# Seven quadrant products for eight in the gate and up projections, with the down projection as a stage behind them

## The chip, the cores and the metric

The kernel runs on one core of one Trainium2 chip. The time is the device time of one execution in microseconds, the median of three runs. The engines are named as in the profile: PE is the matrix engine (PEld its weight load), DVE the vector engine, ACT the scalar engine, POOL the GpSimd engine, SP the engine whose queue issues nearly all the DMAs. The change touches only the last part of the kernel, the feed-forward network; the output projection before it is touched where it hands over.

## What is computed

The block ends with a residual feed-forward network on 1024 tokens (the meta tokens are dropped before it) of width 1024, with an inner width of 2816, in float32:

```
hs  = hs + mixer_block(rmsnorm(hs, norm_mix), ...)
h   = rmsnorm(hs, norm_ffn)
hs  = hs + (silu(h @ w_gate) * (h @ w_up)) @ w_down     # w_gate, w_up: 1024 x 2816, w_down: 2816 x 1024
out = rmsnorm(hs, norm_final)
```

## The kernel before

**Arithmetic.** Each float32 operand of a matmul is held as two tiles, a rounded high part (`wh`, `oph`) and the rest (`wl`, `opl`). One product is three matmuls: high by high, high by low, low by high (`mm3`, which records its matmuls on L196). So a PSUM group of 512 columns that contracts over 1024 takes 8 x 3 = 24 matmuls of 128x128 by 128x512.

**Weights.** `plan` lists the weight blocks in the order of use. `next_w` keeps one block loaded ahead; `load_w` fetches a block of 1024 x 256 in two DMAs of 512 KB into the two `wraw` tiles (L136), rounds it on ACT into `wh` (L138), and subtracts on POOL (first half) and DVE (second half) into `wl` (L139). `wh` and `wl` have two buffers each.

**Hand-over.** In the last quarter of the output projection (`b == 3`, matmuls on L1058, 256 columns) every finished row tile `hs[i]` of 128 tokens gets its sum of squares (ACT, L246) and its scale (POOL, L118 and L119), and DVE writes the scaled copy into an `act` tile (L1034). `norm2_cols` transposes four of these tiles for one of the eight column blocks into a `tp` bank of PSUM (L1042; there are two such banks), and ACT and DVE evict it into a pair `oph`, `opl` (L1044, L1045). The first four row tiles are done inside the output projection; the other four come behind the first 24 matmuls of the feed-forward network.

**Feed-forward.** Eleven steps `s` of 256 inner columns. `gate_up(s)` makes four groups for gate and four for up (two column blocks `j`, two token halves `hh`). The gate groups leave through Silu on ACT into `fsg` (L1089); the up groups are multiplied with these on DVE (L1094), rounded on ACT (L1095) and the rest subtracted on DVE (L1096) into the `act` tiles, which hold all 1024 tokens. `down(s - 1)` follows each `gate_up(s)`: 16 groups of 6 matmuls (L1107), each added on DVE into `hs`, which stays in SBUF (L1109). PSUM groups go round six banks (`pc`: `mm`, `yo`, `ss`, `cb`, `yo`, `yd`). A scheduler sets the order on each engine from the program; `tc.issue_after` holds an instruction behind another.

Of the kernel before, what the change touches and what calls it, by code (L numbers as in the profile page):

```python
# [15 lines left out]
P = 128  # L16
# [41 lines left out]
def tile_hybrid_block(  # L58
# [32 lines left out]
    d_a = dram.tile([KC, P, T], F32, name="d_a")  # L91

# [48 lines left out]

    def next_w(key):

        while plan and len(ready) < 2:
            k, view, lo = plan.pop(0)
            ready.append((k, load_w(view, lo)))
        k, w = ready.pop(0)
        assert k == key, (k, key)
        return w
# [868 lines left out]
    hsp = ctx.enter_context(tc.tile_pool(name="hs", bufs=1))  # L1018
# [3 lines left out]
    h2 = [None] * (2 * KC)  # L1022
    xn = [None] * NTT
    ffp = ctx.enter_context(tc.tile_pool(name="ffp", bufs=2))

    def row_tile():
        return ffp.tile([P, D], F32, name="act", tag="act", bufs=8)

    todo = []

    def norm2_rows(i, added):
        if i:
            with tc.issue_after(added.ins):
                V.tensor_scalar(out=xn[i - 1][0], in0=hs[i - 1], scalar1=xn[i - 1][1], scalar2=None, op0=ALU.mult)  # L1034
        if i < NTT:
            t = row_tile()
            xn[i] = t, rms_stat(t, hs[i], P)

    def norm2_cols(half, k):
        ps = pb("tp")  # L1040
        for i in range(4):
            PE.transpose(ps[:, i * P:(i + 1) * P], xn[4 * half + i][0][:, k * P:(k + 1) * P], ident)  # L1042
        hi, lo = h2[half * KC + k] = op_tile()
        S.activation(out=hi, in_=ps, func=AF.Copy, scale=prm(R_NF, k))  # L1044
        V.scalar_tensor_tensor(out=lo, in0=ps, scalar=prm(R_NF, k), in1=hi.bitcast(F32),  # L1045
                               op0=ALU.mult, op1=ALU.subtract)

    for b in range(4):
        wh, wl = next_w(f"o{b}")
        for i in range(NTT):  # L1050
            ps = pc()
            sl = slice(i % 4 * P, (i % 4 + 1) * P)
            if b == 3 and i == 6:
                todo = list(range(KC))
            for k in range(KC):
                mh, ml = mop[i // 4 * KC + k]
                for q_, (a, bb) in enumerate(((mh, wh), (mh, wl), (ml, wh))):
                    PE.matmul(ps[:, :256], lhsT=a[:, sl], rhs=bb[:, k, :], start=(k == 0 and q_ == 0),  # L1058
                              stop=(k == KC - 1 and q_ == 2))
                if todo and k % 2:  # L1060
                    norm2_cols(0, todo.pop(0))
# [5 lines left out]
    todo = list(range(KC))  # L1067


    def gate_up(s):  # L1070
        res = [[row_tile().bitcast(F32R) for _ in range(2)] for _ in range(2)]
        sgs = []
        for key in ("wg", "wu"):
            wh, wl = next_w(f"{key}{s}")
            for hh in range(2):
                ts = halves(hh)
                for j in range(2):
                    js = slice(j * P, (j + 1) * P)
                    ps = pc()
                    o = h2[hh * KC:(hh + 1) * KC]  # L1080
                    mm3(ps, [wh[:, k, js] for k in range(KC)], [wl[:, k, js] for k in range(KC)],
                        [t[0] for t in o], [t[1] for t in o])
                    if todo:
                        with tc.issue_after(last_mm[0].ins):
                            while todo:
                                norm2_cols(1, todo.pop(0))
                    if key == "wg":
                        sg = ffp.tile([P, 512], F32, name="fsg", bufs=6)
                        S.activation(out=sg, in_=ps, func=AF.Silu)  # L1089
                        sgs.append(sg)  # L1090
                        continue
                    sg = sgs.pop(0)
                    ah, al_ = res[j]
                    V.tensor_tensor(out=sg, in0=ps, in1=sg, op=ALU.mult)  # L1094
                    S.copy(out=ah[:, ts], in_=sg)  # L1095
                    V.tensor_tensor(out=al_[:, ts], in0=sg, in1=ah[:, ts].bitcast(F32), op=ALU.subtract)  # L1096
        return res

    def down(s, res, after=None):
        wh, wl = next_w(f"wd{s}")  # L1100
        for i in range(NTT):
            sl = slice(i * P, (i + 1) * P)
            for t0, n in HALF:
                ps = pc()
                for k in range(2):
                    for q_, (a, bb) in enumerate(((res[k][0], wh), (res[k][0], wl), (res[k][1], wh))):
# [76 lines left out]
```

## Time and profile before

| | |
|---|---|
| median of three runs | 2297.45 us (2295.74 to 2298.12) |
| the profiled execution's own time | 2297.74 us |
| its span, first to last instruction | 2295.9 us |
| PE / DVE / ACT / POOL busy | 2228.8 / 1383.9 / 764.4 / 846.0 us |
| mean granted PE clock | 0.991 of full speed |

A busy share is a mean over the whole span. The feed-forward network is the last third of the span, from 1550.67 us on; the part of it that changes runs to 2243.97 us, the start of the last down step, which stays as it is.

### The profile page before, as it was taken

Reading aid. Unit: us, or ns where it says so; the run is one execution under the profiler, and the core shown is the slowest. Engines: PE = TensorE matmul, PEld = TensorE weight load, DVE = VectorE, ACT = ScalarE, POOL = GpSimd, SP = SyncE. Lnnn points to the kernel's source line nnn. Section 1 sums busy time; section 2 is a strip of 40 time slices with the busy share of each in tenths; the row PEclk is TensorE's granted clock in tenths of the full one; section 3 lists DMA queues with packets and bytes.
Section 4 is the critical chain, followed back from the end, with each engine's and each line's share of the span. In section 5 each row is a group of like instructions: output and inputs, shape, how many; then the busy total and the mean of one; then the engine's idle time right before and its main releaser. Section 6 shows DMA issues by size and latency. Waiting matters only on the chain.

```text
span 2295.9 us, 30987 instructions
## 1 busy us (share of the span) xinstructions
PE 2228.8 (97%) x12103; PEld 1903.6 (83%) x12103; DVE 1383.9 (60%) x1726; ACT 764.4 (33%) x1386; POOL 846.0 (37%) x729
## 2 busy tenths in 40 slices
PE   7999999999999999988999999999999999999998
PEld 7999999999997766665677788998888888888886
DVE  4389898997871587887997664533332333433236
ACT  6333342322322454545555462223111111111112
POOL 3374664821202586867785510111010110101102
PEclk9999999999999999999999999999999999999999
DMA  4222222232236675746753752411111111111111
GB/s 140 85 76 67 83 70 71 86 119 99 89 109 202 195 209 164 226 142 209 229 169 119 241 159 84 147 38 52 41 56 37 55 39 53 55 37 56 37 55 73
DMA packets 223162, 245.29 MB, mean 107 GB/s; under 512 B 19113, under 2 KB 174361, under 8 KB 223017
## 3 DMA queue, kind: packets, MB, share of 16 engines
q1 hardware_dynamic: 210200, 221.89, 31.3%
q10 hardware_dynamic: 12816, 21.44, 2.5%
q8 instruction: 95, 1.56, 0.3%
q14 instruction: 51, 0.41, 0.1%
HBM read 174.23 MB, written 69.04 MB: 106 GB/s over the span
## 4 chain that ended last, share of the span: by engine, by line
PE 48%; DMA 2%; DVE 2%; ACT 1%; POOL 1%; issue 1%; SPq 0%; POOLq 0%; DVEq 0%; ACTq 0%
PE yo L196 11%; PE mm L196 9%; PE ss L196 4%; PE yd L196 4%; PE cb L196 4%; PE yo L1107 3%; PE ss L1107 2%; PE cb L1107 2%; PE yd L1107 2%; DMA wraw<-d_vn 1%; PE mm L1107 1%; PE yo L1058 1%; PE cb L1058 1%; PE ss L1058 1%; PE mm L1058 1%
## 5 line engine op out<-in xcount | busy, mean ns | idle before, releaser
L139 POOL TENSOR_TENSOR wl<-wraw,wh 128x1024 fp32r<-128x1024 f32 (+1 forms) x103 | 249.9, 2436 | 1080.0 <-ACT wh L138 1079.8
L196 PE MATMUL mm<-hnh,wh 128*128 128x352 f32 (+4 forms) x1208 | 410.6, 340 | 14.9 <-ACT w L553 13.5
L196 PE MATMUL mm<-hnh,wl 128*128 128x352 f32 (+4 forms) x1208 | 403.8, 334 | 2.8 <-POOL wl L139 2.8
L196 PE MATMUL mm<-hnl,wh 128*128 128x352 f32 (+4 forms) x1208 | 405.8, 336 | 0.4 <-DVE hnl L378 0.4
L138 ACT CAST wh<-wraw 128x1024 fp32r<-128x1024 f32 (+1 forms) x172 | 175.0, 1042 | 420.3 <-PE yd L1107 175.5
L139 DVE TENSOR_TENSOR wl<-wraw,wh 128x1024 fp32r<-128x1024 f32 x69 | 139.2, 2020 | 252.6 <-ACT wh L138 247.8
L196 PEld LDWEIGHTS mm<-hnh,wh 128*128 128x128 f32 x1208 | 228.3, 189 | 29.9 <-ACT w L553 17.5
L474 DVE SCALAR_TENSOR_TENSOR acc<-ap,pr,acc 128x1024 f32<-128x1024 f32 x192 | 247.5, 1289 | 6.3
L196 PEld LDWEIGHTS mm<-hnh,wl 128*128 128x128 f32 x1208 | 228.3, 189 | 12.9 <-POOL wl L139 3.4
L196 PEld LDWEIGHTS mm<-hnl,wh 128*128 128x128 f32 x1208 | 228.2, 189 | 9.8 <-issue 1.2
L474 DVE SCALAR_TENSOR_TENSOR acc<-xp,pr,acc 128x1040 f32<-128x1040 f32 x120 | 156.6, 1305 | 4.0
L196 PE MATMUL mm<-oph,wh 128*128 128x512 f32 x344 | 139.5, 405 | 11.9 <-ACT w L656 9.9
L272 PE MATMUL mm<-wh,hnh 128*128 128x256 f32 x512 | 144.7, 283 | 5.1 <-ACT w L275 5.1
L272 PE MATMUL mm<-wl,hnh 128*128 128x256 f32 x512 | 144.6, 283 | 0.0
L272 PE MATMUL mm<-wh,hnl 128*128 128x256 f32 x512 | 144.5, 283 | 0.0
L196 PE MATMUL mm<-opl,wh 128*128 128x512 f32 x344 | 137.1, 398 | 3.0 <-DVE opl L623 3.0
L196 PE MATMUL yo<-oph,wh 128*128 128x512 f32 x352 | 139.0, 395 | 0.0
L196 PE MATMUL yo<-opl,wh 128*128 128x512 f32 x352 | 138.9, 395 | 0.0
L196 PE MATMUL yo<-oph,wl 128*128 128x512 f32 x352 | 138.8, 394 | 0.0
L196 PE MATMUL mm<-oph,wl 128*128 128x512 f32 x344 | 136.7, 397 | 0.0
L758 POOL TENSOR_SCALAR_AFFINE_SELECT sel<-adh 128x512 fp32r<-128x512 f32 x128 | 98.7, 792 | 70.8 <-ACT wh L138 41.6
L513 POOL TENSOR_TENSOR tap<-tap 128x1024 f32<-128x1024 f32 x40 | 96.1, 2403 | 34.4 <-ACT tap L509 33.3
(316 smaller groups left out, 4938.8 us busy)
## 6 DMA issues: line engine op xcount, KB each, us to landing
wraw<-in_w_in_dram SPq DMA_DIRECT2D x72, 512.0 KB, 3.7
xc<-d_x SPq DMA_DIRECT2D x64, 256.0 KB, 3.5
wraw<-in_w_gate_dram SPq DMA_DIRECT2D x22, 512.0 KB, 4.7
wraw<-in_w_up_dram SPq DMA_DIRECT2D x22, 512.0 KB, 3.8
wraw<-in_w_down_dram SPq DMA_DIRECT2D x22, 512.0 KB, 3.7
d_x<-xa ACTq DMA_DIRECT2D x16, 520.0 KB, 2.6
d_sz<-w ACTq DMA_DIRECT2D x64, 128.0 KB, 2.1
d_xt<-xt SPq DMA_DIRECT2D x32, 256.0 KB, 3.3
```

The lines of the kernel that those rows point to most:

```text
L138: S.copy(out=h3[:, sl], in_=r3)
L139: (V if lo[i] == "v" else GP).tensor_tensor(out=l3[:, sl], in0=r3, in1=h3[:, sl].bitcast(F32), op=ALU.subtract)
L196: tie(PE.matmul(out_, **kw))
L272: PE.matmul(ps[:, :256], lhsT=a[:, sl], rhs=bb[:, k, :], start=(k == 0 and q_ == 0), stop=(k == KC - 1 and q_ == 2))
L474: V.scalar_tensor_tensor(out=out_ if last else acc, in0=sl(k), scalar=w(k), in1=acc, op0=ALU.mult, op1=ALU.add)
L513: GP.tensor_tensor(out=t, in0=t, in1=part, op=ALU.add)
L758: GP.affine_select(out=dst, in_=hbc(src, self.c, h0, 4, P, P), pattern=[[0, 4], [-1 if back else 1, P]], compare_op=ALU.is_ge, fill=0.0, b ...
L1058: PE.matmul(ps[:, :256], lhsT=a[:, sl], rhs=bb[:, k, :], start=(k == 0 and q_ == 0), stop=(k == KC - 1 and q_ == 2))
L1107: PE.matmul(ps, lhsT=a[:, sl], rhs=bb[:, k, t0:t0 + n], start=(k == 0 and q_ == 0), stop=(k == 1 and q_ == 2))
```

## The change

Gate and up. Step 0 is still computed with 24 matmuls for each group (`gate_up_plain`). In steps 1 to 10 a weight block is cut into four quadrants (`A11`, `A21`, `A12`, `A22`: two column blocks by two halves of the contraction) and the normalized activations into four (`B11`, `B21`: token half 0, `B12`, `B22`: token half 1, by the halves of the contraction). Strassen's scheme in Winograd's form gives the four results from seven products of quadrants, each contracting over 512, so of 4 x 3 = 12 matmuls (`wino`). It needs four sums of weight quadrants (`S1` to `S4`, made anew for each block in `load_wino`, all four by POOL), four of activation quadrants (`T1` to `T4`, made once at the hand-over in `norm2_second` and `norm2_last`), and sums of the products, which DVE adds as it evicts them (`plus`). Seven pairs are rounded and split for each block where `load_w` split 2 halves of a block.

Down. The gated result goes to memory (`d_act`); the loads of `wd` move in `plan` behind all gate and up blocks; `load_act` reads the result back in pieces of 128x512 and splits it there. `hs` is written to memory unscaled (`d_hs`), scaled in place for the transposes, its place given to other tiles, and it is read back for the down stage.

```diff
+    def load_wino(view):
+        fa = fa_box[0]
+        raws = []
+        for i in range(2):
+            raw = wts.tile([P, 1024], F32, name="wraw", tag="wraw", bufs=2)
+            r3 = raw.rearrange("p (a b) -> p a b", b=256)
+            SP.dma_start(out=r3, in_=view[:, 4 * i:4 * i + 4, :])
+            raws.append(r3)
+        a11, a21, a12, a22 = (raws[h][:, :, j * P:(j + 1) * P] for h in range(2) for j in range(2))
...
+            if name in ("S3", "A22", "S4"):
+                pair = tuple(fa.tile([P, 512], F32R, name=n_, bufs=3) for n_ in ("yah", "yal"))
+            else:
+                pair = slots.pop(0)
+            h, l = (k4(t) for t in pair)
+            S.copy(out=h, in_=src)
+            eng.tensor_tensor(out=l, in0=src, in1=h.bitcast(F32), op=ALU.subtract)
+            res[name] = h, l
+
+        s1 = k4(fa.tile([P, 512], F32, name="s1", bufs=1))
+        split_q("A11", a11, V)
+        split_q("A12", a12, V)
+        GP.tensor_tensor(out=s1, in0=a21, in1=a22, op=ALU.add)
+        GP.tensor_tensor(out=a21, in0=a11, in1=a21, op=ALU.subtract)
+        GP.tensor_tensor(out=a11, in0=s1, in1=a11, op=ALU.subtract)
+        split_q("S2", a11, V)
+        split_q("S1", s1, GP)
+        GP.tensor_tensor(out=a12, in0=a12, in1=a11, op=ALU.subtract)
+        split_q("S3", a21, V)
+        split_q("A22", a22, GP)
+        split_q("S4", a12, GP)
+        return res
...
-        add_plan(f"wg{i}", w_gate[0], 256 * i, LOD)
-        add_plan(f"wu{i}", w_up[0], 256 * i, LOD)
-        if i:
-            plan_down(i - 1)
-    plan_down(NFF // 2 - 1)
+        add_plan(f"wg{i}", w_gate[0], 256 * i, None if i else LOD)
+        add_plan(f"wu{i}", w_up[0], 256 * i, None if i else LOD)
+    for i in range(NFF // 2):
+        plan_down(i)
...
         if i:
             with tc.issue_after(added.ins):
-                V.tensor_scalar(out=xn[i - 1][0], in0=hs[i - 1], scalar1=xn[i - 1][1], scalar2=None, op0=ALU.mult)
+                V.tensor_scalar(out=hs[i - 1], in0=hs[i - 1], scalar1=rsx[i - 1], scalar2=None, op0=ALU.mult)
         if i < NTT:
...
+            SP.dma_start(out=d_hs[i], in_=hs[i])
+            rsx[i] = rms_stat(fx.tile([P, D], F32, name="t2", bufs=2), hs[i], P)
...
+    def norm2_second(k):
+        ps = norm2_cols(1, k)
+        b12 = B["B12", k] = split_cols(ps, k, x_pair("x", 4))
+        h11, l11 = (t.bitcast(F32) for t in B["B11", k])
+        t1 = fx.tile([P, 512], F32, name="t1", bufs=2)
+        V.scalar_tensor_tensor(out=t1, in0=ps, scalar=prm(R_NF, k), in1=h11, op0=ALU.mult, op1=ALU.subtract)
+        V.tensor_tensor(out=t1, in0=t1, in1=l11, op=ALU.subtract)
+        B["T1", k] = split_t(op_tile(), t1, GP)
+        ps = norm2_cols(1, k + 4)
+        B["B22", k] = split_cols(ps, k + 4, op_tile())
...
+        V.scalar_tensor_tensor(out=t2, in0=ps, scalar=prm(R_NF, k + 4), in1=t1, op0=ALU.mult, op1=ALU.subtract)
+        B["T2", k] = split_t(x_pair("y", 8), t2, GP)
+        t3 = fx.tile([P, 512], F32, name="t3", bufs=2)
+        V.scalar_tensor_tensor(out=t3, in0=ps, scalar=prm(R_NF, k + 4), in1=b12[0].bitcast(F32), op0=ALU.mult,
+                               op1=ALU.subtract)
+        V.tensor_tensor(out=t3, in0=t3, in1=b12[1].bitcast(F32), op=ALU.subtract)
+        B["T3", k] = split_t(x_pair("y", 8), t3, GP)
+
+    def norm2_last(k):
+        t2 = t2f[k + 1]
+        h21, l21 = (t.bitcast(F32) for t in B["B21", k])
+        GP.tensor_tensor(out=t2, in0=h21, in1=t2, op=ALU.subtract)
+        V.tensor_tensor(out=t2, in0=t2, in1=l21, op=ALU.add)
+        B["T4", k] = split_t(x_pair("x", 4), t2, V)
...
+    def act_out(s, j, hh, ps_or_sum, sg):
+        V.tensor_tensor(out=sg, in0=ps_or_sum, in1=sg, op=ALU.mult)
+        SP.dma_start(out=d_act[2 * s + j, :, halves(hh)], in_=sg)
...
+    def wino(key, emit):
+        w = next_w(key)
+
+        def prod(a, b):
+            ps = pc()
+            h, l = w[a]
+            for k in range(4):
+                bh, bl = B[b, k]
+                for q_, (x_, y_) in enumerate(((h, bh), (h, bl), (l, bh))):
+                    matmul(ps, lhsT=x_[:, k, :], rhs=y_, start=(k == 0 and q_ == 0), stop=(k == 3 and q_ == 2))
+            return ps
...
+        S.copy(out=u, in_=prod("A11", "B11"))
+        emit(0, 0, plus(prod("A12", "B21"), u))
+        plus(prod("S2", "T2"), u, u)
+        u3 = plus(prod("S3", "T3"), u)
+        ps = prod("S1", "T1")
+        emit(1, 1, plus(ps, u3))
+        plus(ps, u, u)
+        emit(1, 0, plus(prod("A22", "T4"), u3, u3))
+        emit(0, 1, plus(prod("S4", "B22"), u, u))
...
+    def load_act(s):
+        res = {}
+        for hh in range(2):
+            for j in range(2):
+                h, l = res[j, hh] = op_tile()
+                SP.dma_start(out=l.bitcast(F32), in_=d_act[2 * s + j, :, halves(hh)])
+                S.copy(out=h, in_=l.bitcast(F32))
+                (V, GP)[j].tensor_tensor(out=l, in0=l.bitcast(F32), in1=h.bitcast(F32), op=ALU.subtract)
+        return res
...
-    prev = None
     for s in range(NFF // 2):
-        res = gate_up(s)
-        if prev is not None:
-            down(s - 1, prev)
-        prev = res
-    down(NFF // 2 - 1, prev, final_norm)
+        nxt = load_act(s + 1) if s + 1 < NFF // 2 else None
+        down(s, res, None if nxt else final_norm)
+        res = nxt
```

The scheduler places the added work. On DVE at the hand-over, from the scaling of the sixth row tile on, the rows before were these (`hs_14371` is the last row tile):

```order
L1034 TENSOR_SCALAR act<-hs_14370,rs 128x1024
L1045 SCALAR_TENSOR_TENSOR opl<-tp,pr,oph 128x512
L1034 TENSOR_SCALAR act<-hs_14371,rs 128x1024
L139 TENSOR_TENSOR wl<-wraw,wh 128x1024
L1045 SCALAR_TENSOR_TENSOR opl<-tp,pr,oph 128x512 x8
L139 TENSOR_TENSOR wl<-wraw,wh 128x1024
```

The same place after the change (`hs_14376` is the last row tile; `t_15437` is a `t1`, `t_15453` a `t2`, `t_15459` a `t3`; `xh`, `xl` are the pair of `B12`):

```order
L141 TENSOR_TENSOR wl<-wraw,wh 128x1024
L1084 TENSOR_SCALAR hs_14376<-hs_14376,rs 128x1024
L1097 SCALAR_TENSOR_TENSOR xl<-tp,pr,xh 128x512
L1117 SCALAR_TENSOR_TENSOR t_15437<-tp,pr,oph 128x512
L1118 TENSOR_TENSOR t_15437<-t_15437,opl 128x512
L1097 SCALAR_TENSOR_TENSOR opl<-tp,pr,oph 128x512
L1125 SCALAR_TENSOR_TENSOR t_15453<-tp,pr,t_15437 128x512
L1128 SCALAR_TENSOR_TENSOR t_15459<-tp,pr,xh 128x512
L1097 SCALAR_TENSOR_TENSOR xl<-tp,pr,xh 128x512
L1130 TENSOR_TENSOR t_15459<-t_15459,xl 128x512
L1117 SCALAR_TENSOR_TENSOR t_15475<-tp,pr,oph 128x512
L1138 TENSOR_TENSOR t_15453<-t_15453,opl 128x512
```

Eight evictions of `tp` in a row have become a series in which a `tp` bank is read by two or three DVE instructions, with additions between SBUF tiles among them; the weight split (L139, now L141) now stands ahead of the scaling of the last row tile. On PE the eight transpose groups of the second half, which stood within the first two PSUM groups of the network, are now spread over its first four, with 0, 9, 16, 7, 11, 7 and 16 matmuls of 512 columns between one and the next.

On the queue of SP, the end of the feed-forward network before (`hs_14364` to `hs_14366` are row tiles):

```order
L136 DMA wraw<-in_w_gate_dram 128x4x256 x2
L136 DMA wraw<-in_w_up_dram 128x4x256 x2
L136 DMA wraw<-in_w_down_dram 128x1024 x4
L1136 DMA out_dram<-hs_14364 128x1024
L1136 DMA out_dram<-hs_14365 128x1024
L1136 DMA out_dram<-hs_14366 128x1024
```

After the change, from the first reads of the gated result to the first five reads of `hs` (`hs_18672` to `hs_18676`):

```order
L1244 DMA opl<-d_act 128x512 x8
L138 DMA wraw<-in_w_down_dram 128x1024
L1165 DMA d_act<-fsg 128x512
L138 DMA wraw<-in_w_down_dram 128x1024
L1244 DMA opl<-d_act 128x512 x4
L138 DMA wraw<-in_w_down_dram 128x1024
L1165 DMA d_act<-fsg 128x512
L1255 DMA hs_18672<-d_hs 128x1024
L1165 DMA d_act<-fsg 128x512
L1255 DMA hs_18673<-d_hs 128x1024
L1165 DMA d_act<-fsg 128x512
L1255 DMA hs_18674<-d_hs 128x1024
```

The twelve reads for the first three down steps have been moved ahead of the last four writes of `d_act`; the reads of `hs` stand between and behind those writes.

## Rows read from the trace of the kernel before

**Rows 1.** The page, parts 1 and 2: span, busy PE, granted clock.

```profile
span 2295.9 us, 30987 instructions
...
PE 2228.8 (97%) x12103; PEld 1903.6 (83%) x12103; DVE 1383.9 (60%) x1726; ACT 764.4 (33%) x1386; POOL 846.0 (37%) x729
...
PEclk9999999999999999999999999999999999999999
```

**Rows 2.** Chain of work in order of time from 1500 us: start, length, what.

```profile
1599.95 5.60 PE mm L196 x24
...
1639.15 5.60 PE yo L196 x24
1666.53 5.60 PE mm L196 x24
```

**Rows 3.** Busy time by stretch: one gate_up, then one down; clock, DMA share, GB/s.

```profile
1599.95:1644.75 44.80, 44.80 (x193) 35.90 (x193) 10.07 (x10) 8.65 (x13) 4.80 (x2) 1.00 0.14 47
1644.75:1666.53 21.78, 21.78 (x97) 18.02 (x97) 13.69 (x18) 2.45 (x3) 2.40 (x1) 1.00 0.16 49
```

**Rows 4.** Groups by form, 1700 us to the end: busy, mean ns | idle before.

```profile
L196 PE MATMUL yo<-oph,wh 128*128 128x512 f32 x200 | 78.8, 394 | 0.0
...
L1096 DVE TENSOR_TENSOR act<-fsg,act 128x512 fp32r<-128x512 f32 x35 | 24.1, 688 | 17.8 <-ACT act L1095 17.8
...
L1095 ACT CAST act<-fsg 128x512 fp32r<-128x512 f32 x35 | 21.6, 618 | 121.9 <-DVE fsg L1094 121.9
...
L1094 DVE TENSOR_TENSOR fsg<-yo,fsg 128x512 f32<-128x512 f32 x17 | 11.8, 692 | 41.2 <-PE yo L196 41.2
```

**Rows 5.** Groups by form on POOL, whole run: operations on 512 elements.

```profile
L679 POOL TENSOR_TENSOR xw<-xt,wd 128x512 f32<-128x512 f32 x56 | 64.8, 1164 | 12.3 <-ACT xt L720 8.7 <-DMA xt<-d_xt 3.5
...
L959 POOL TENSOR_TENSOR lcs<-lcs,sq 128x512 f32<-128x512 f32 x14 | 21.8, 1558 | 1.9 <-ACT sq L955 1.0
```

**Rows 6.** Line L139 from 1560 us: duration ns min/median/max.

```profile
L139 POOL TENSOR_TENSOR wl<-wraw,wh x31: 2399/2402/2419, 1578.5 to 2245.0; 128x1024 fp32r<-128x1024 f32 x31
L139 DVE TENSOR_TENSOR wl<-wraw,wh x31: 2035/2520/2579, 1579.9 to 2246.0; 128x1024 fp32r<-128x1024 f32 x31
```

**Rows 7.** Timeline at one weight split: start, length, engine, line.

```profile
2245.03 2.40 POOL L139 TENSOR_TENSOR wl<-wraw,wh 128x1024 fp32r<-128x1024 f32 x1 [20.09 <-ACT wh L138]
...
2245.99 2.52 DVE L139 TENSOR_TENSOR wl<-wraw,wh 128x1024 fp32r<-128x1024 f32 x1
```

**Rows 8.** Timeline of the hand-over: transposes, evictions, the weight split on DVE.

```profile
1556.49 1.22 DVE L139 TENSOR_TENSOR wl<-wraw,wh 128x1024 fp32r<-128x1024 f32 x1
...
1560.39 0.60 PE L1042 MATMUL tp<-ident,act 128*128 128x128 f32 x4
...
1562.55 0.42 PEld L1042 LDWEIGHTS tp<-ident,act 128*128 128x128 f32 x4 [0.40 <-DVE opl L1045]
...
1563.25 0.69 ACT L1044 ACTIVATE oph<-tp,pr 128x512 fp32r<-128x512 f32 x1 [0.86 <-PE tp L1042]
...
1563.97 0.75 DVE L1045 SCALAR_TENSOR_TENSOR opl<-tp,pr,oph 128x512 fp32r<-128x512 f32 x1 [0.80 <-ACT oph L1044]
```

**Rows 9.** Waits from 1540 to 1600 us: total us, times, longest.

```profile
PEld tp L1042 <- DVE opl L1045: 1.4, 5, 0.4
```

**Rows 10.** DMA issues from 1500 us: KB each, median us to landing.

```profile
wraw<-in_w_gate_dram SPq DMA_DIRECT2D x22, 512.0 KB, 4.7
...
out_dram<-hs SPq DMA_DIRECT2D x7, 512.0 KB, 2.6
```

**Rows 11.** DMA issues from 1380 to 1560 us, and the rate in 40 slices.

```profile
GB/s 58 62 58 211 80 58 58 5 226 124 58 60 58 222 73 0 0 0 279 396 415 198 4 219 14 4 0 0 223 14 0 0 4 233 0 4 0 0 0 162
...
hs<-in_x_dram SPq DMA_DIRECT2D x8, 512.0 KB, 7.6
```

**Rows 12.** Chain from 2230 us: one PSUM group of the last down step.

```profile
2245.35 1.36 PE cb L1107 x6
```

More of the change, by code (lines that the diff above doesn't have):

```diff
@@ L91, in tile_hybrid_block @@
     d_a = dram.tile([KC, P, T], F32, name="d_a")
+    d_act = dram.tile([NFF, P, T], F32, name="d_act")
+    d_hs = dram.tile([NTT, P, D], F32, name="d_hs")
     ones = const.tile([P, P], F32, name="ones")
@@ L1041, in norm2_cols @@
         for i in range(4):
[L1042 to L1045, printed above, removed]
-                               op0=ALU.mult, op1=ALU.subtract)
+            PE.transpose(ps[:, i * P:(i + 1) * P], hs[4 * half + i][:, k * P:(k + 1) * P], ident)
@@ new lines, in norm2_cols, with split_cols, norm2_first, split_t @@
+        return ps
+    def split_cols(ps, k, pair):
+        S.activation(out=pair[0], in_=ps, func=AF.Copy, scale=prm(R_NF, k))
+        V.scalar_tensor_tensor(out=pair[1], in0=ps, scalar=prm(R_NF, k), in1=pair[0].bitcast(F32),
+                               op0=ALU.mult, op1=ALU.subtract)
+        return pair
+    def norm2_first(k):
+        B["B11" if k < 4 else "B21", k % 4] = split_cols(norm2_cols(0, k), k, op_tile())
+    t2f = {}
+    def split_t(pair, t, eng):
+        S.copy(out=pair[0], in_=t)
+        eng.tensor_tensor(out=pair[1], in0=t, in1=pair[0].bitcast(F32), op=ALU.subtract)
+        return pair
@@ L1097, in gate_up @@
-        return res
+                            for k in range(4):
+                                norm2_second(k)
+                        hs_ctx.close()
+                        fa_box.append(fa_ctx.enter_context(tc.tile_pool(name="fa", bufs=1)))
+                    if u_ == 0:
+                        sgs[j, hh] = fa_box[0].tile([P, 512], F32, name="fsg", bufs=4)
+                        S.activation(out=sgs[j, hh], in_=ps, func=AF.Silu)
+                    else:
+                        act_out(s, j, hh, ps, sgs.pop((j, hh)))
@@ new lines, in tile_hybrid_block, with emit_gate @@
+    gate_up_plain(0)
+    for k in range(4):
+        norm2_last(k)
+    for s in range(1, NFF // 2):
+        sgs = {}
+        def emit_gate(j, hh, r):
+            sgs[j, hh] = fa_box[0].tile([P, 512], F32, name="fsg", bufs=4)
+            S.activation(out=sgs[j, hh], in_=r, func=AF.Silu)
+        wino(f"wg{s}", emit_gate)
+        wino(f"wu{s}", lambda j, hh, r: act_out(s, j, hh, r, sgs.pop((j, hh))))
+    def load_act(s):
+        res = {}
+        for hh in range(2):
+            for j in range(2):
[3 more added lines that the diff above has]
+                (V, GP)[j].tensor_tensor(out=l, in0=l.bitcast(F32), in1=h.bitcast(F32), op=ALU.subtract)
+        return res
@@ L1099, in down @@
+    res = load_act(0)
+    fa_ctx.close()
+    fx_ctx.close()
+    ffp = ctx.enter_context(tc.tile_pool(name="ffp", bufs=2))
+    hs = [ffp.tile([P, D], F32, name=f"hs{i}", bufs=1) for i in range(NTT)]
+    for i in range(NTT):
+        SP.dma_start(out=hs[i], in_=d_hs[i])
     def down(s, res, after=None):
```

74 lines of the change are left out of this document (39 added, 35 removed).

## The prediction, made before the changed kernel ran

> **What bounds the kernel now.** I read the page first: PE is busy 97% of the span, and its granted clock stands at the top step in every slice [rows 1]. A busy share may hide waits, so the next view is the chain of work in order of time. Through the whole feed-forward network it consists of PE alone, one PSUM group after the other: a gate or up group of 24 matmuls takes 5.60 us, and eight of them follow one another without a gap, from 1599.95 to 1644.75 us, with the down step filling the time up to the next one at 1666.53 us [rows 2]. The stretches say the same: in a gate_up of 44.80 us PE is busy for 44.80 us at clock 1.00 (the 2.4 GHz level), while DVE works for 10.07, ACT for 8.65, POOL for 4.80 us and the DMA engines are 14% busy [rows 3]. The groups by form give PE no idle time at all ahead of its matmuls [rows 4]. So in this part a matmul less is time less, as long as what the change adds elsewhere stays under PE.
>
> Two durations follow. A gate or up matmul costs 5.60 / 24 = 0.2333 us; a down matmul 21.78 / 96 = 0.2269 us [rows 2, 3]. Both have 512 columns; they differ in where the operands lie (in gate and up the moving operand comes from the `op` tiles, in down from `wh` and `wl`).
>
> **What is removed.** Ten steps, gate and up: 20 weight blocks. A block took 4 groups x 24 = 96 matmuls and takes 7 x 12 = 84. That is 20 x 12 = 240 matmuls less, at 0.2333 us 56.0 us. The new products are 20 x 84 = 1680 matmuls, and I take the same 0.2333 us for them. Three of the seven read their moving operand (`T2`, `T3`, `T4`) from tiles that did not exist; if these go at the rate of down, 720 x 0.0064 = 4.6 us more are gained, if all do, 10.8 us. Down keeps its 1056 matmuls, but its stationary operand now lies in the `op` tiles; I take no change, with 1056 x 0.0064 = 6.8 us of loss as the bound.
>
> The Trainium skill ("TensorE: Matmul & The Clock Gate", section "Back-to-back issue gap") gives N / 2.4 GHz and 2.5 ns between matmuls at full clock, 215.8 ns for 512 columns, by which the removal would bring 51.8 us. Neither 233.3 nor 226.9 ns agrees with it, and the measured spacing decides.
>
> **What is added inside a block of weights**, which PE now needs 7 x 2.80 = 19.6 us for. ACT: seven roundings, one copy from PSUM, and for gate four Silus, at about 0.62 us [rows 4] at most 7.4 us. POOL: four sums and three rests on 512 elements. The trace has no such sums on quadrants (rows of 128 with gaps between them); operations on 512 elements take 1.16 to 1.56 us [rows 5], so 8 to 11 us. DVE: seven additions out of PSUM, four rests, for up four gating products, each 0.69 us [rows 4]: 7.6 or 10.4 us. All of it lies beside PE; the six PSUM banks give an eviction five further products, 14 us, of delay before PE has to stop. I cost it at nothing; what it costs if that cover goes is the business of the third and fourth rival.
>
> The weights have to come round too. A raw tile is only free for the next load when the rest of `S4` is taken. Load 4.7 us [rows 10], then five POOL operations up to the difference for `S4`, its rounding, its rest: 4.7 + 5 x 1.56 + 0.62 + 1.56 = 14.7 us with the longer POOL time, under 19.6 us.
>
> **DMA.** The gated result is written (44 x 256 KB) and read again, `hs` too (8 + 8 x 512 KB): 31 MB, spread over some 690 us about 45 GB/s on top of 47 to 49 [rows 3], where the same queue has run at 415 [rows 11]. On the queue of SP the reads for the first three down steps stand ahead of the last writes, so no down step waits for a round trip through memory. Taken as hidden.
>
> **The hand-over, the one place where I expect a price.** Today the eight transpose groups of the second half make PE wait 1.4 us in all, for the DVE eviction that frees one of the two `tp` banks [rows 8, 9]. After the change a pair of groups (one `k`) needs of DVE five instructions that read PSUM, at 0.75 us [rows 8], and three additions between SBUF tiles at 0.69 us (one of them from `norm2_last`, which the scheduler draws forward): 5.8 us. From the second to the last transpose group PE has 66 matmuls, 15.4 us, and six groups at some 0.35 us, together 17.5 us; the last group must wait for three pairs, 17.4 us and the first eviction on ACT, 0.69 us. Alone that is close to even, say 1.5 us of stall because the order of the evictions does not fit exactly. But POOL has four operations for each pair, 4.7 to 6.2 us out of 5.8, and DVE and POOL get in each other's way. A split on DVE takes 1.22 us by itself [rows 8], 2.52 us beside POOL [rows 6]: it began 0.96 us after POOL's and ended 1.08 us after POOL was done [rows 7]. So it waited for the whole of the other. Nine DVE additions with both inputs in SBUF can meet that; lower bound nothing, upper bound 9 x 1.56 = 14.0 us. I take under half a POOL operation each, 4 us in all. With the 1.5 us, and without the 1.4 us of today: +4.1 us. The last row tile is scaled behind the weight split and behind the write of `d_hs` (2.6 us to landing for such a write [rows 10]); the first is the later of the two, +0.3 us.
>
> **Entering down.** The last six `hs` reads are issued behind the last gating product. Eight such loads took 7.6 us to land when issued together [rows 11], and PE can run six groups of 1.36 us, 8.2 us, before the first addition must be done [rows 12]. I take +0.5 us, bounds 0 and 5.
>
> **Sum.** Against the profiled execution's own 2297.7 us (span 2295.9 and 1.8 around it): 2297.7 - 56.0 + 4.1 + 0.3 + 0.5 = 2246.6. That execution lay 0.3 us above the median, so 2246 us, 2.2% less. A measurement here can tell from no change what is over 0.2%, 4.6 us.
>
> **Rivals.**
>
> 1. The forecast, with the matmul rates and hand-over anywhere in their bounds but not all bad: 2236 (new products partly at 0.2269 us, no stall) to 2257 us (hand-over at +15). Chance 0.78.
>
> 2. The hand-over costs far more, because the first Strassen blocks must wait for the `T` pairs. POOL has 16 operations there and 7 for the first block, 27 to 36 us, plus DVE's turns; it has about 41 us, from 9 us into the network to the end of step 0 at 50 us. For it: that is nearly all the time there is. Against it: `S1` is not needed until 11 us into the block, `T4` until 14. Price 10 to 20 us more, 2257 to 2268 us. Chance 0.13.
>
> 3. The weights come round too slowly: the 14.7 us above grow past 19.6, which takes loads or POOL sums longer by 4.9 us a block. For it: POOL is blocked by DVE too. Against it: five of 20 us are spare. Each microsecond beyond costs 20 us; the gain is gone at 22.4 us a block. 2268 to 2297 us, chance 0.05.
>
> 4. Slower than before: DVE stands behind POOL in every block. For a gate and an up block DVE has 14 additions out of PSUM, 9.7 us, and 12 instructions with two SBUF inputs of 0.69 us and a wait w; PE takes 39.2 us. DVE becomes the bound when w exceeds 1.77 us, and the gain is gone at 44.8 us, w = 2.24 us. Should POOL need for 512 elements in pieces of 128 what it needs for 1024 in a row, 2.40 us [rows 6], and DVE wait for all of it each time: 46.8 us, +7.6 for each of ten pairs, 2322 us. Against it: the rows on 512 elements end at 1.56 us, and POOL is not always at work when DVE comes. Chance 0.04. The Trainium skill ("SBUF — State Buffer", section "Who interferes with whom") has the rule: a DVE instruction with two SBUF inputs and a POOL instruction that reads SBUF lock each other out for a whole instruction. By that rule, with which 2.52 beside 1.22 us agrees, this rival would be as priced only if POOL were always first.
>
> That the seven products do not replace the eight on the path can be left out: PE has no gap in which the removed matmuls could have been free [rows 4].
>
> **Numbers.** Range 2236 to 2260 us: it leaves out the better part of rival 2 and rivals 3 and 4, less than 2 in 10. Faster by over 0.2%: cases 1 and 2 and nearly all of 3, 0.95; within 0.2%: 0.01; slower: 0.04.
>
> **What would show it.** Right: products of 12 matmuls at 2.80 us, seven to a block, blocks 19.6 us apart, PE idle only at the hand-over and at the door to down; down groups at 1.36 us. The gaps at the hand-over should have DVE as releaser and `tp` as the tile. Wrong: gaps of PE in every block, released by POOL or ACT on `yah`, `wl` (rival 3) or by DVE on a PSUM bank (rival 4); POOL sums on quadrants above 1.6 us; a product well off 2.80 us.

## The result, and the profile of the changed kernel

The changed kernel takes 2271.1 us (median of four runs, 2270.57 to 2272.18) against 2296.66 us before; the ratio is 0.9889, 95% interval 0.9872 to 0.9906. So it is faster, by 25.6 us and not by the 51 that were forecast, and outside the range (2236 to 2260 us).

The page, parts 1 and 2 (answers to [rows 1]):

```profile
span 2269.8 us, 31785 instructions
...
PE 2174.4 (96%) x11863; PEld 1854.1 (82%) x11863; DVE 1525.8 (67%) x1932; ACT 824.8 (36%) x1522; POOL 1060.0 (47%) x887
...
PEclk9999999999999999999999999999999999999999
```

Busy time by stretch (columns as in [rows 3]): step 0, then the 20 Strassen blocks, then down up to its last matmul:

```profile
1551.00:1606.30 55.30, 49.87 (x231) 39.30 (x230) 42.98 (x49) 25.82 (x43) 37.93 (x26) 1.00 0.17 52
1606.30:2006.10 399.80, 390.55 (x1681) 313.74 (x1679) 189.19 (x250) 113.86 (x198) 195.13 (x135) 1.00 0.26 80
2006.10:2261.40 255.30, 247.87 (x1056) 198.98 (x1056) 174.90 (x224) 55.12 (x90) 65.87 (x52) 1.00 0.33 113
```

Before, PE was busy for the whole of such stretches [rows 3]. Now it is idle for 5.4, 9.2 and 7.4 us in them, at clock 1.00 throughout. The waits of PE from 1600 to 2030 us (total us, times, longest) name one line of DVE, the addition of products out of PSUM (the three largest of ten rows); below them DVE's own largest wait:

```profile
PE yo L243 <- DVE mu L1210: 2.5, 3, 1.1
PE mm L1266 <- DVE mu L1210: 2.4, 1, 2.4
PE yo L1266 <- DVE mu L1210: 2.3, 1, 2.3
...
DVE wl L173 <- ACT wh L172: 194.3, 57, 6.7
```

The chain of work (answers to [rows 2, 12]): a product with an `op` tile, two with `y` tiles (`T2`, `T3`), and a down group:

```profile
1606.43 2.80 PE mm L243 x12
...
1612.03 2.74 PE ss L243 x12
1614.77 2.72 PE cb L243 x12
...
2027.57 1.40 PE yd L1266 x6
```

The span against the forecast of 2244.8 us, term by term:

| | forecast | measured | off by |
|---|---|---|---|
| begin of the network, against 1550.67 | 0 | 1551.01 | +0.3 |
| step 0 (before: 1599.95 - 1550.67 = 49.3) | 53.7 | 55.3 | +1.6 |
| 1680 matmuls of the products | 391.9 | 390.6 | -1.3 |
| PE waiting in the blocks | 0 | 9.2 | +9.2 |
| PE waiting at the entry to down | 0.5 | 7.4 | +6.9 |
| 1056 matmuls of down | 239.6 | 247.9 | +8.3 |

Together +25.0, which is the whole miss. Three terms make it: two kinds of waits, and the rate of down.

**Where the waits in the blocks come from.** They begin behind the tenth block, at 1803 us, and then come once a block, some 0.9 us each. DVE is the releaser (the engine whose instruction ended the wait), but it is not busy: it stands in line itself. One round of the weights in the time line of SP, ACT, POOL, DVE and PE (start, length, what; in brackets the idle time before and its releaser):

```profile
1929.12 0.37 SPq L157 DMA_DIRECT2D wraw<-in_w_up_dram  x1
1932.87 0.62 ACT L172 CAST wh<-wraw 128x512 fp32r<-128x512 f32 x1 [6.44 <-DMA wraw<-in_w_up_dram]
1933.40 1.14 ACT L172 CAST yah<-wraw 128x512 fp32r<-128x512 f32 x2
1934.09 3.00 POOL L173 TENSOR_TENSOR yal<-wraw,yah 128x512 fp32r<-128x512 f32 x2 [5.89 <-ACT yah L172]
1937.12 0.38 SPq L157 DMA_DIRECT2D wraw<-in_w_up_dram  x1
1941.42 1.29 POOL L179 TENSOR_TENSOR s<-wraw 128x512 f32<-128x512 f32 x1 [4.32 <-DMA wraw<-in_w_up_dram]
1945.81 0.62 ACT L172 CAST wh<-wraw 128x512 fp32r<-128x512 f32 x1 [2.45 <-POOL wraw L181]
1946.47 1.11 DVE L173 TENSOR_TENSOR wl<-wraw,wh 128x512 fp32r<-128x512 f32 x1 [2.61 <-ACT wh L172]
1947.51 0.68 DVE L1210 TENSOR_TENSOR mu<-mm,mu 128x512 f32<-128x512 f32 x1
1948.33 0.47 PE L243 MATMUL mm<-oph,wh 128*128 128x512 f32 x1 [0.88 <-DVE mu L1210]
1948.89 0.68 DVE L173 TENSOR_TENSOR yal<-wraw,yah 128x512 fp32r<-128x512 f32 x1
1949.64 8.55 SPq L157 DMA_DIRECT2D wraw<-in_w_gate_dram  x2
```

The first raw tile of the next block is loaded from 1929.12 on and lands at 1932.87. ACT has waited 6.44 us for it, to round `A11`, and only behind that come the roundings of `A22` and `S4` of the block before, for which everything had been there since 1928. With their rests (POOL, to 1937.09) the second raw tile comes free, and its load starts at 1937.12, 8.0 us behind the first. It lands at 1941.42; then come three sums, `S2`'s rounding, its rest on DVE, two additions, the rest of `S3`, and the first raw tile is free again at 1949.6. The round: 3.7 load, 4.3 to the second load, 4.3 load, 4.4 sums, 3.8 to the end, 20.5 us, where PE needs 19.4 to 19.6. DVE stands in it, with `S2`'s rest ahead of an addition that frees a PSUM bank, and there PE waits.

The order on ACT in the program shows it (`yah` are `S3`, `A22`, `S4`; the first `wh` behind a `yah` is `A11` of the next block):

```
L172 CAST yah<-wraw 128x512
L172 CAST wh<-wraw 128x512
L172 CAST yah<-wraw 128x512 x2
```

**At the entry** the same thing holds DVE for longer, since the block behind is the first one of down:

```profile
2001.43 1.05 ACT L140 CAST wh<-wraw 128x1024 fp32r<-128x1024 f32 x1 [4.08 <-DMA wraw<-in_w_down_dram]
...
2002.52 1.23 DVE L141 TENSOR_TENSOR wl<-wraw,wh 128x1024 fp32r<-128x1024 f32 x1 [9.62 <-ACT wh L140]
...
2006.07 0.68 DVE L1210 TENSOR_TENSOR mu<-ss,mu 128x512 f32<-128x512 f32 x1
```

DVE waits 9.62 us for the second half of down's first weights, with the additions of the last block's products behind it, and needs until 2020 us to catch up.

**At the hand-over**, DVE and PE:

```profile
1576.68 1.78 DVE L1138 TENSOR_TENSOR t<-t,opl 128x512 f32<-128x512 f32 x1 [1.19 <-POOL t L1137]
1578.38 0.74 DVE L1097 SCALAR_TENSOR_TENSOR opl<-tp,pr,oph 128x512 fp32r<-128x512 f32 x1
...
1579.70 0.74 DVE L1128 SCALAR_TENSOR_TENSOR t<-tp,pr,xh 128x512 f32<-128x512 f32 x1
...
1580.59 0.63 PE L1092 MATMUL tp<-ident,hs 128*128 128x128 f32 x4 [2.83 <-DVE t L1128]
```

The addition for `T4` (L1138), which nothing needs for another 40 us, waits 1.19 us for POOL and then takes 1.78 us instead of the 0.68 that such an addition takes beside an idle POOL. Behind it stand the three readings of a `tp` bank, and PE waits 2.83 us for the last of them.

The theory, then: the order on ACT puts two loads in series into the weights' round; what the round lacks is paid in the blocks and at the entry. `T4`'s early additions pay at the hand-over. For the rate of down, the place of the tiles. The rivals are told with the experiments. In these, stretches of the network are compared where the total would mislead: it began between 1547.0 and 1554.2 us in the profiles, although nothing ahead of it was changed in most of them. Experiments 1 to 4 ran on one chip, 5 to 8 on a second, 9 to 12 on a third.

### The profile page after: what moved, and what is told of

It reads as the page before. It is cut to its first block, busy times and chain, and to the rows that moved or that the text cites. A ratio compares the mean times of both kernels' runs of the same rounds, so it can differ in the third digit from the quotient of the medians.

```text
span 2269.8 us, 31785 instructions
## 1 busy us (share of the span) xinstructions
PE 2174.4 (96%) x11863; PEld 1854.1 (82%) x11863; DVE 1525.8 (67%) x1932; ACT 824.8 (36%) x1522; POOL 1060.0 (47%) x887
## 4 chain that ended last, share of the span: by engine, by line
PE 30%; POOL 7%; issue 7%; DMA 5%; DVE 3%; ACT 2%; SPq 0%; POOLq 0%; DVEq 0%; ACTq 0%
PE yo L243 5%; PE mm L243 4%; PE yo L1266 3%; PE ss L243 3%; PE yd L243 2%; PE cb L243 2%; PE mm L1266 2%; PE yd L1266 2%; PE cb L1266 2%; PE ss L1266 2%; POOL yal L173 1%; DMA wraw<-d_vn 1%; POOL wraw L180 1%; PE yo L1152 1%; POOL wraw L184 1%
## 5 line engine op out<-in xcount | busy, mean ns | idle before, releaser
L141 POOL TENSOR_TENSOR wl<-wraw,wh 128x1024 fp32r<-128x1024 f32 (+1 forms) x83 | 201.9, 2443 | 545.9 <-ACT wh L140 523.1
L140 ACT CAST wh<-wraw 128x1024 fp32r<-128x1024 f32 (+1 forms) x132 | 134.4, 1042 | 239.3 <-PE mm L243 54.1
L173 DVE TENSOR_TENSOR wl<-wraw,wh 128x512 fp32r<-128x512 f32 x60 | 60.8, 1014 | 194.3 <-ACT wh L172 194.3
L172 ACT CAST wh<-wraw 128x512 fp32r<-128x512 f32 x60 | 37.2, 621 | 224.9 <-DMA wraw<-in_w_up_dram 114.6
L141 DVE TENSOR_TENSOR wl<-wraw,wh 128x1024 fp32r<-128x1024 f32 x49 | 91.6, 1872 | 37.6 <-ACT wh L140 32.0
L173 POOL TENSOR_TENSOR yal<-wraw,yah 128x512 fp32r<-128x512 f32 x40 | 55.4, 1395 | 116.4 <-ACT yah L172 110.3
L243 PE MATMUL mm<-oph,wh 128*128 128x512 f32 x224 | 92.1, 411 | 15.1 <-ACT w L703 10.9
L319 PEld LDWEIGHTS mm<-wh,hnh 128*128 128x128 f32 x512 | 96.3, 188 | 5.9 <-ACT w L322 5.8
L805 POOL TENSOR_SCALAR_AFFINE_SELECT sel<-adl 128x512 fp32r<-128x512 f32 x128 | 99.3, 798 | 0.1
```

Of the source, the lines that this page charges most:

```text
L140: S.copy(out=h3[:, sl], in_=r3)
L141: (V if lo[i] == "v" else GP).tensor_tensor(out=l3[:, sl], in0=r3, in1=h3[:, sl].bitcast(F32), op=ALU.subtract)
L172: S.copy(out=h, in_=src)
L173: eng.tensor_tensor(out=l, in0=src, in1=h.bitcast(F32), op=ALU.subtract)
L243: tie(PE.matmul(out_, **kw))
L805: GP.affine_select(out=dst, in_=hbc(src, self.c, h0, 4, P, P), pattern=[[0, 4], [-1 if back else 1, P]], compare_op=ALU.is_ge, fill=0.0, b ...
```

## Experiments

**1. Only the order on ACT.** In `load_wino`, and likewise for the first cast in `load_w` behind the blocks:

```diff
-            S.copy(out=h, in_=src)
+            if name == "A11" and last_cast:
+                with tc.issue_after(last_cast[0].ins):
+                    cast = S.copy(out=h, in_=src)
+            else:
+                cast = S.copy(out=h, in_=src)
+            last_cast[:] = [cast]
```

> One rule is added to the changed kernel: on ACT, the rounding of the next block's first quadrant (A11), and of the first half of the first down block, is held behind the rounding of S4 of the block before, instead of standing ahead of A22 and S4. Theory (the weights' round takes 20.5 us a block because two loads stand in it one after the other: ACT waits for the next block's first load with A22 and S4 of this block queued behind it, so the second raw tile comes free a load too late): the round falls under 19.6 us, the ten waits of about 0.9 us (9.2 us) in the blocks go, and of the 7.4 us of waiting at the entry to down most of what DVE's late weight split causes, 3 to 6 us: 2256 to 2260 us. Rival A (POOL's quadrant sums and DVE's locks on them set the round, whatever the order on ACT): no change, 2269 to 2273 us. Rival B (only the blocks gain, the entry keeps its 7.4 us): 2262 us.

Measured: 2246.45 us (2239.71 to 2252.84), ratio to before 0.9784 (0.9758 to 0.9810). PE does not wait in the blocks, nor at the entry:

```profile
1602.30:1990.30 388.00, 388.00 (x1682) 314.71 (x1681) 217.28 (x259) 124.35 (x207) 198.47 (x139) 1.00 0.28 90
1990.30:2237.10 246.80, 246.73 (x1057) 199.20 (x1055) 166.92 (x214) 48.82 (x82) 59.50 (x49) 1.00 0.30 106
```

Beside the first profile's rows the blocks take 11.8 us less and down 8.5 us less. That profile is from another set of runs; on the same chip, experiment 2 below has the old order at 2262.38 us, 16 us more, and experiment 4 the new order with the edit of experiment 2, 10 us less than that. Rivals A and B fall: POOL and DVE do the same work in both, and DVE shows even more busy time in the blocks (217.3 us against 189.2). The rule binds ACT alone, but the scheduler moved DVE's rest of `A11` two to four places back with it, so this run by itself does not separate the two orders; that the length of the round follows the number of loads is shown by experiments 11 and 12. The total is below the expected 2256 to 2260 by 10 us; 4 of them are the network's earlier start (1547.0), the rest lies in PE's own time (388.0 for 390.6, 246.7 for 247.9) and in the entry, where all of the 7.4 us went and not 3 to 6.

**2. `op` tiles 64 bytes lower.** A tile of 64 bytes is put ahead of their pool.

```diff
+        ctx.enter_context(tc.tile_pool(name="pad", bufs=1, side="right")).tile([P, 16], F32, name="pad")
         opp_box.append(ctx.enter_context(tc.tile_pool(name="ops", bufs=16, side="right")))
```

> The changed kernel with every op tile moved down by 64 bytes in each partition, nothing else. These tiles begin at 64 bytes behind a multiple of 128; the tiles of T2, T3, T4 and of the weights begin at a multiple of 128. Theory (a 512-column matmul costs 0.2333 to 0.235 us where an operand lies in an op tile, 0.2269 to 0.228 us elsewhere, because of where these tiles begin): the groups of down fall from 1.40 to 1.36 us (1056 matmuls, 6.8 to 8.3 us), the products with op tiles from 2.80 to 2.73 us (80 of them, 5 us, partly lost again in waits for the weights), and the products of the earlier projections gain too: 2255 to 2264 us. Rival (the rate hangs on which operand is held and which moves, or on the order of the three matmuls, and not on the place): down stays at 1.40 us a group, the products at 2.80, 2269 to 2273 us.

Measured: 2262.38 us (2259.2 to 2266.89), as the theory had it, but not for its reason. Down groups still take 1.40 us. What shrank are the waits: 3.6 us in the blocks and 4.7 at the entry. Experiment 5 comes to the same time without the edit, though on another chip.

**3. Down apart, without Strassen.** All eleven steps are `gate_up_plain`, and all weight blocks are loaded and split as in step 0 (`LOD` in `plan`).

> All eleven steps of gate and up with 24 matmuls for each group as before, down as a stage of its own behind them through memory as in the changed kernel; T1 to T3 are still made at the hand-over and not used. Theory (the entry's 7.4 us come mostly from DVE, late behind the Strassen blocks' weights; down pays for its operand in op tiles; the hand-over pays for the T sums): 2296.7 + 8.3 (down's rate) + 4 to 6 (hand-over, start) + 0 to 3 (entry) = 2309 to 2314 us, PE without waits inside the blocks. Rival (the entry's price is that of the round trip through memory): the same gaps of 7 us at the entry, 2316 to 2319 us. If down's groups took 1.36 us here, the rate would not be a matter of the stationary operand's tile: 2302 to 2307 us.

Measured: 2304.18 us, ratio 1.0033 (1.0020 to 1.0046). The three stretches again:

```profile
1549.40:1599.10 49.70, 49.03 (x230) 39.33 (x229) 31.24 (x39) 22.16 (x35) 25.54 (x17) 1.00 0.24 80
1599.10:2044.70 445.60, 445.60 (x1921) 359.40 (x1920) 82.61 (x65) 68.86 (x90) 54.52 (x25) 1.00 0.24 78
2044.70:2291.30 246.60, 246.60 (x1057) 199.39 (x1055) 163.38 (x209) 49.93 (x81) 59.37 (x47) 1.00 0.29 102
```

No wait at the entry: the way through memory costs nothing here, so the 7.4 us belong to what stands ahead of it, the late weights. Down's 246.6 us are 7.0 above the 239.6 that its rate of before would give. Less than expected in total, because the hand-over has only 0.7 us of waits here (the `T4` additions are missing; `T1` to `T3` are made), and because gate and up take 0.2321 us a matmul instead of 0.2333: a quarter of their moving operands (`B12`) now lies in `x` tiles.

**4. Experiments 1 and 2 together.**

> The order of the first experiment and the op tiles of the second together. If both theories hold and the two add: 2242 to 2252 us, with no waits of PE in the blocks (whose products then take about 19.1 us for seven, which the weights' round of some 15 us still leaves room for). If the order alone holds, as the first experiment; if the place alone, as the second; if the weights' round is bound by POOL and DVE, the place gains only in down, 2262 to 2266 us.

Measured: 2252.16 us, 5.7 above experiment 1. From the network's begin to the end it is 697.2 us where experiment 1 has 698.6; the difference lies ahead of it (1554.2 against 1547.0 us). The 64 bytes bring 1.4 us in the network at most.

**5. The changed kernel again,** on the chip of the next three runs.

> The changed kernel itself once more, as the yardstick for the others on this chip. Theory (the second experiment's 8 us were not the place of the tiles but that a weight load took 0.3 to 0.4 us less in that run than in the first profile of the changed kernel, and the round holds two loads in series): the round follows the load's time, 20.2 us a block with loads of 3.4 to 3.6 us, 20.6 with 3.7 to 4.2, so 2260 to 2272 us, and the waits of PE add up to 8 to 17 us accordingly. Rival (64 bytes of place were worth 8 us): 2269 to 2273 us, waits of 16 us, whatever the loads take.

Measured: 2262.95 us, ratio 0.9858 (0.9840 to 0.9876), with no edit at all. Waits of 2.8 us in the blocks and 7.0 at the entry; a load of the up weights lands after a median 3.8 us here, as in experiment 2, against 4.0 in the first profile, and the first wait comes at 1922 us instead of 1803. So the changed kernel's time moves by 8 us from one set of runs to another. Of the 9.9 us between the two profiles, the blocks take 7.1 us less, most of it waits, and down 5.4 us less, of which 4.3 are PE's own time: its groups take 1.37 us here and not 1.40, with the same tiles. Against that the network begins 2.6 us later. The waits fit a round without reserve and a shorter load; how much of them is the load was not separated from the rest, and the two rates of down stay open.

**6. `T4` held back,** with the order of experiment 1.

```diff
-        GP.tensor_tensor(out=t2, in0=h21, in1=t2, op=ALU.subtract)
-        V.tensor_tensor(out=t2, in0=t2, in1=l21, op=ALU.add)
+        with tc.issue_after(tail[1].ins):
+            GP.tensor_tensor(out=t2, in0=h21, in1=t2, op=ALU.subtract)
+        with tc.issue_after(tail[0].ins):
+            V.tensor_tensor(out=t2, in0=t2, in1=l21, op=ALU.add)
```

(`tail` holds the last `T3` subtraction on DVE and the last rest on POOL.)

> The first experiment's order, and the making of T4 (one POOL and one DVE addition for each of four pairs) held behind the last subtraction for T3 on DVE and the last rest of the T's on POOL. Theory (5.4 us of waiting at the hand-over come from DVE, which stands at T4's additions for a POOL addition and then for the lock, with evictions of the two tp banks behind them): the waits in step 0 fall from 5.4 to under 1.5 us, 2240 to 2243 us where the first experiment gives 2246. Rival (DVE and POOL have too much to do there in any order): the waits move to other transposes or to the first Strassen block, whose sixth product needs T4; 2245 to 2248 us.

Measured: 2241.76 us (2240.28 to 2244.53), ratio to before 0.9763 (0.9745 to 0.9780); 21 us under the changed kernel on the same chip. It is the best of all versions.

```profile
1553.90:1603.70 49.80, 49.15 (x231) 39.39 (x230) 37.57 (x46) 22.59 (x37) 35.96 (x25) 1.00 0.12 43
1603.70:1991.70 388.00, 388.00 (x1682) 314.69 (x1681) 219.27 (x264) 126.97 (x212) 200.61 (x141) 1.00 0.29 92
```

Step 0 takes 49.8 us, as before the change (49.3), with 0.65 us of waits. And the weights now wait for PE, not PE for them; the rounding of `A22` on ACT stands until the product that read its buffer is done:

```profile
1911.32 0.62 ACT L181 CAST yah<-wraw 128x512 fp32r<-128x512 f32 x1 [4.92 <-PE ss L253]
```

**7. Other tiles for down,** with the order of experiment 1.

```diff
-                h, l = res[j, hh] = op_tile()
+                h, l = res[j, hh] = op_tile() if s < 3 else tuple(
+                    ffp.tile([P, 512], F32R, name=n_, bufs=12) for n_ in ("ah", "al"))
```

> The first experiment's order, and from the fourth down step on the gated result lies in other tiles, at 100 to 152 KB of a partition, where the op tiles lie at 164 to 229 KB. Theory (a 512-column matmul is slower by 0.0064 us where an operand lies in the high tiles): down groups of the fourth and later steps take 1.36 us instead of 1.40, 8 steps of 96 matmuls, 4.9 us: 2240 to 2242 us where the first experiment gives 2246. Rival (the rate is that of a held operand read in rows of 512 elements, or of the order of the three matmuls, wherever it lies): 1.40 us a group, 2245 to 2248 us.

Measured: 2250.66 us, slower than expected by either. It is compared with experiment 1 on another chip, but the rows of this run alone show both parts. The rate does change where the tiles do, but by little; the chain at the passage from the third to the fourth step:

```profile
2063.82 1.37 PE yo L1277 x6
2065.20 1.38 PE ss L1277 x6
2066.58 1.36 PE cb L1277 x6
2067.94 1.36 PE yo L1277 x6
```

From the starts, 228.9 ns a matmul before and 226.6 behind, 2.3 ns and not 6.4: 1.8 us over 768 matmuls. The loss is a wait that the edit brought: the first additions of down wait for `hs`, and the chain there runs over a write of `d_act` and a read of `hs` that now stand later in SP's queue:

```profile
PE ss L1277 <- DVE hs L1279: 4.8, 1, 4.8
```

**8. Order, late `T4` and other tiles together.**

> The order on ACT, the late T4 and the other tiles for down together. If all three theories hold: 2235 to 2238 us where the first experiment gives 2246; each that fails gives back its 4.9 us.

Measured: 2246.11 us, ratio 0.9783 (0.9767 to 0.9800): the wait for `hs` (3.8 us here) takes more than the tiles give.

**9 and 10. Doubled loads,** in the changed kernel and in that of experiment 6.

```diff
-            SP.dma_start(out=r3, in_=view[:, 4 * i:4 * i + 4, :])
+            for _ in range(2):
+                SP.dma_start(out=r3, in_=view[:, 4 * i:4 * i + 4, :])
```

> The changed kernel, with every load of a Strassen weight block into a raw tile done twice, one behind the other; the result is the same. It makes each load some 3.8 us longer. Theory (two loads in series in the round of 20.2 to 20.6 us): the round grows by 7.6 us to about 28 us a block, 8.6 us above what PE needs, in some 19 blocks: 2415 to 2445 us. Rival (the round is one load and POOL's and DVE's work): 24.2 us a block, 2340 to 2365 us. If the loads were hidden, no change.

> The same doubled loads in the kernel with the order on ACT and the late T4. Theory (one load in the round: 4 us of load, 7.3 of POOL's five operations up to the sum for S4, 3.7 for the last rounding and the two rests, 15.0 us; with the doubled load 18.8, still under the 19.4 that PE needs for a block): 2242 to 2262 us, hardly a wait in the blocks. Rival (the loads are still in series, the order only moved the wait elsewhere): 2400 us or more.

Measured: 2288.07 and 2285.26 us; both expectations fail. In the first of them the scheduler itself now puts `A22` and `S4` ahead of the next `A11` (perhaps since it counts the added loads), so both have the same order on ACT, and this pair by itself tells nothing of the order. For the second the expected sum was too low. From one `S1` sum to the next (1920.13 to 1941.30 us) it is 7.3 us for five POOL operations, 2.4 until ACT has rounded `A22`, which stands behind a Silu that waits for DVE, 2.6 for the rests, 8.9 for two loads: 21.2 us. With each load done once it would be some 4.4 less, 16.8 us (an estimate: half of the 8.9 taken off): under PE's 19.4, with 2.6 us to spare.

**11 and 12. The old order fixed,** loads once and twice. `A22` and `S4` of a block are written behind the next block's `A11`:

```diff
+        first = split_q("A11", a11, V)
+        if pending:
+            pending.pop()(first)
+        a12, a22 = load(1)
...
+        def rest(ins):
+            late_q[:] = [ins]
+            split_q("A22", a22, GP)
+            split_q("S4", a12, GP)
+
+        pending.append(rest)
```

> The program is written so that ACT's order of the changed kernel is fixed: A22 and S4 of a block are rounded behind the rounding of the next block's first quadrant, whatever the scheduler thinks of the loads. Loads are done once. Theory and rivals alike: about the time of the changed kernel on this chip, 2258 to 2272 us, a round of 20.0 to 20.7 us a block. It is the yardstick for the next one.

> The same fixed order with every load of a Strassen weight block done twice, one behind the other. In the earlier two runs with doubled loads the scheduler had chosen the same order on ACT for both, A22 and S4 first, and both took 21.7 us a block; here it can't. Theory (two loads in series in the round): the round grows by both second loads, 3.8 and 3.8 to 4.4 us, to 28 to 29 us a block, 2405 to 2445 us. Rival (one load counts, the order is without effect): 21.7 us a block as in those two, 2280 to 2295 us, or 24 to 25 us, 2330 to 2365.

Measured: 2263.45 and 2392.53 us. The `S1` sums of the 20 blocks, first with loads once, then with loads twice (duration in ns, first and last start):

```profile
L194 POOL TENSOR_TENSOR s<-wraw x20: 1272/1290/1302, 1585.9 to 1980.8; 128x512 f32<-128x512 f32 x20
```

```profile
L194 POOL TENSOR_TENSOR s<-wraw x20: 1277/1288/1295, 1585.1 to 2109.1; 128x512 f32<-128x512 f32 x20
```

A round is (1980.8 - 1585.9) / 19 = 20.8 us and (2109.1 - 1585.1) / 19 = 27.6 us: 6.8 more, 3.4 for each of two added loads. (The first round of each, 30.3 and 36.2 us, lies in step 0; without it the means are 20.3 and 27.1, as far apart.) PE's granted clock is 0.94 of full speed in the blocks of the second run and 1.00 in those of the first; the round runs over SP, ACT, POOL and DVE. With the other order, doubled loads cost 2288.07 us (experiment 9), 104 us less; the 2285.26 of experiment 10 hold the late `T4` as well. So in the order of the changed kernel both loads stand in the round, in the other order one.

## Why the prediction was wrong

**The weights' round: the step that failed.** "Load 4.7 us, then five POOL operations up to the difference for `S4`, its rounding, its rest: 14.7 us." It followed one tile's own chain and left out the queue on ACT, in which the roundings of this tile stand behind a rounding that waits for the next block's other tile. With that, 20.5 us. The third rival named this ("the weights come round too slowly", 2268 to 2297 us, chance 0.05), and 2271 lies in it; its chance was judged against five spare microseconds that were not there. In the order that the sum had in mind the round is some 16.8 us (experiment 10): the five POOL operations took 7.3 us where it has 7.8, but the rounding came 2.4 us behind them and the rests took 2.6. So its 14.7 were short as well, but still under what PE needs.

**The sign was misread in advance.** Gaps with DVE on a PSUM bank were to mean the fourth rival, DVE behind POOL's locks. They came, and meant the third: DVE was idle for 194 us in front of the weight rests, and the bank's addition stood behind one. The wait w on which the fourth rival turned was small. In the blocks of the changed kernel three of the four rests and the gating products on DVE took 1.02 and 0.97 us in the mean:

```profile
L173 DVE TENSOR_TENSOR wl<-wraw,wh 128x512 fp32r<-128x512 f32 x57 | 58.3, 1024 | 192.5 <-ACT wh L172 192.5
L1164 DVE TENSOR_TENSOR fsg<-mu,fsg 128x512 f32<-128x512 f32 x36 | 35.1, 974 | 0.9
```

Beside the 0.69 us that the prediction took for them, w is some 0.3 us, where 1.77 would have made DVE the bound.

**The entry to down: +0.5 forecast, 7.4 measured.** The step looked at the reads of `hs` and of the gated result. These cost nothing (experiment 3). What stood there was DVE's split of down's first weights, late for the same reason; the order of experiment 1 alone removes it all. The 7.6 us for eight loads were misread too: they are the median from issue to landing of one such load, not the time until all eight are in. In the changed kernel PE waited 0.5 us for them; in experiments 7 and 8, where the reads of `hs` stand behind all writes of `d_act`, it is where PE waits.

**Down's rate: the unit price that was mis-sized.** "I take no change, with 6.8 us of loss as the bound": 8.3 measured in that run, of which 176 groups at 1.40 instead of 1.36 are 7.0. The runs of experiments 5 to 12 have 1.37 with the same tiles. By place, experiment 7 shows 2.3 ns a matmul in one run; what makes the rest, 228.9 ns in some runs and 233.4 in others at clock 1.00, stays open. The Trainium skill ("TensorE: Matmul & The Clock Gate", section "Back-to-back issue gap") has 215.8 ns by its formula for a single matmul's gap and about 131 ns as its sustained figure for 512 columns. Neither agrees: no product and no group of down here comes below 226.6 in the mean.

**The products: right.** 390.6 us against 391.9; without waits 388.0, as the lower rate for `T2`, `T3` and `T4` had been bounded (-4.6).

**The hand-over: right in kind.** +6.0 us measured against +4.4, inside its bounds; the second rival's 10 to 20 us did not come. The price was put on locks spread over nine additions; experiment 6 shows that nearly all of it hung on four additions that were early. The Trainium skill ("SBUF — State Buffer", section "Who interferes with whom") has a lock between a DVE instruction with two SBUF inputs and a POOL instruction that reads SBUF, held for a whole instruction; 1.78 us beside 0.68 agrees.

**DMA and the preparation's amount of work: right.** ACT, POOL and DVE did the same work in experiment 1 with no wait of PE. One sign of being wrong came without deciding anything: of POOL's four sums, two took more than 1.6 us in the median (1.62 and 1.73), the other two 1.29.

Experiment 1, with the two kinds of waits gone, comes to 2246.45 us where 2246 was forecast. That is luck in part, since three terms offset one another: down's rate costs 7, the products give 4 more than forecast, and the network began 4 us earlier.

## What to carry to other kernels

When a change adds a preparation that runs in a ring (its buffers are loaded again only when its last step has read them), the length of the ring is to be taken along every in-order queue that it passes: an instruction that waits for the next round's load holds up all of this round's that stand behind it, and then a ring that seems to hold one load holds two. Where a trace names a releaser, ask first whether that engine was busy or itself in line; here DVE freed the banks late because it waited for ACT, which waited for a DMA. An operation that nothing needs for long, drawn forward by a scheduler, costs what stands behind it.

## What was not expected of the hardware

The same 128x128 by 128x512 matmul was spaced at 226.6, 228.9 or 233.4 ns in stretches with the clock at 1.00: within one run by the tile of its held operand (experiment 7) or of its moving one (products of 2.72 and 2.80 us), and between sets of runs with the same tiles. And a kernel whose weights come round without reserve showed 2271.1 us in one set of runs and 2262.95 in another, while the kernel before moved by 1.4 us (2296.66 and 2295.28). Of the 9.9 us between the profiles of these two, some 6 are waits for the weights and some 4 the two rates of down.
